# Three mixed pairs of K tiles instead of two in the MLP's up products

## The chip, the cores and the metric

The kernel runs on one core of one Trainium2 chip. The metric is the device time of one execution in microseconds (us); the time of a kernel is the median of its runs. Three runs of the kernel before took 2447.22, 2447.89 and 2448.03 us, so its time is 2447.89 us. One more execution was recorded by the hardware profiler; it is the source of every row of the profile below.

## The reference

A decoder of two layers over 256 tokens of width 2048, all in float32. Each layer has an attention, an MLP and a gated embedding step, each behind an RMSNorm. The change touches the MLP alone:

```python
hn = rmsnorm(h, mlp_norm_g[i])
h = h + jnp.square(jax.nn.relu(hn @ mlp_w1[i])) @ mlp_w2[i]
```

`mlp_w1[i]` is 2048 x 8192 and `mlp_w2[i]` is 8192 x 2048. The first product is called the ups here, the second the downs.

## The kernel before

**Every product in three.** A float32 operand is split into a part rounded to the matmul's format (hi) and the remainder (lo). A product of two operands is the sum of three matmuls: hi x hi, lo x hi, hi x lo (`terms`). In the rows below, `xa` holds the split activations of one K tile (128 features by 256 tokens, hi and lo side by side), `whi` and `wlo` the split weights of one chunk, `h` the split hidden activations. TensorE (PE) takes 128 tokens of an activation tile as its stationary operand and streams 512 weight columns through it, so each matmul row reads 128x512. Three such matmuls are one block product, called a triple from here on.

**Chunks.** Weights come as chunks of 128x1024 (512 KB), two K tiles by 512 columns. `Program.run` walks a list of chunks and writes the instructions of each engine in order. Of each chunk SyncE (SP) issues the load into `raw` (4 buffers), ScalarE (ACT) casts it to `whi` (line 243, 6 buffers), and VectorE (DVE) subtracts to get `wlo` (line 251, 5 buffers). Casts are written up to four chunks ahead of the matmuls, subtractions three (`SPLIT_AHEAD`). Each engine works its list in order, so an instruction that waits holds everything behind it on that engine. A subtraction waits for its cast, and for PE to be done with the chunk five places back, whose `wlo` buffer it takes; a load waits until the buffer of the load four places back was read for the last time.

**The MLP.** `mlp` cuts the 8192 hidden columns into 4 blocks (`NFB`) of four groups of 512. The first two groups of block 0 are made by `ups` on their own, chunk by chunk (`token_major`, line 589). All other groups are made two at a time by `up_mixed` (`pair_major`, line 493): seven calls in a layer, fourteen in the kernel. The calls of block 0 stand alone, the others come in two right behind each other, and downs stand between the blocks.

**Plain and mixed pairs.** A call of `up_mixed` handles groups 0 and 1, each with eight chunks, one for each pair of K tiles. A pair that is plain costs two chunks of four triples: two K tiles by two halves of the tokens, for each group. A pair in `MIXED` costs seven triples for both groups together, after Strassen's scheme in Winograd's form. It is worked as four items named a, b, t and u of two, one, two and two triples. Items a and b are loaded chunks. Item t takes the sum `ts` that DVE makes of both chunks (line 531), and item u what DVE makes of them in place in b's `raw` buffer (lines 536 and 537); both are then cast and subtracted like a loaded chunk, b only in half. The buffer of a is free again after line 536, that of b after the subtraction of u. The mixed items also need sums of the pair's activations, the tile `xf`, made once in a layer for each mixed pair by `x_forms` (ACT at 553 and 563, DVE at 556 to 559 and 566; `all_forms`). Four banks of PSUM collect the extra products of a call; after the last mixed item `sums` combines them (lines 778 to 783), and each group's `done` adds its own bank (line 790) before the squared ReLU. `turned` then brings the rows into feature order through DRAM: DVE transposes blocks (line 697), SP writes `dU` and reads it back into `w` in four parts, ACT and DVE split it to `h` (lines 757 and 759).

**The order.** `order` in `up_mixed` is written by hand. Before, with M for a mixed pair, 0 and 1 for a plain chunk of that group, a call reads 0 0 M 0 1 0 M 0 0 1 1 1 1 1: twenty items. `all_forms` is started behind the last chunk of the first `ups`.

**A scratch tile.** `rsh` (32 partitions by 256) is scratch of the rotary embedding in three places; it comes from the pool `tmp`, which stays open throughout.

Of the kernel before, what the change touches and what calls it, by code (L numbers as in the profile page):

```python
# [10 lines left out]
F32 = mybir.dt.float32  # L11
F32R = mybir.dt.float32r
# [3 lines left out]
P = 128  # L16
D = 2048
T = 256
# [16 lines left out]
DMA_AHEAD = 7  # L35
SPLIT_AHEAD = 3
RAW_BUFS, HI_BUFS, LO_BUFS = 4, 6, 5
MIXED = (2, 5)

G_ATTN, G_MLP, G_PLE, G_KV, G_FIN = 0, 2, 4, 6, 7  # L40

# [119 lines left out]
def kernel(ctx: ExitStack, tc: tile.TileContext, a: dict, out: bass.AP):  # L161
# [386 lines left out]
    def x_forms(k, gi, to):  # L548


        u = [tmp.tile([P, T], F32, tag="sq", name="sq", bufs=3) for _ in range(3)]
        for i in range(2):
            nc.scalar.activation(u[i], x[k + i], AF.Identity, scale=gain(gi, k + i))
        yield
        a, b, s = u
        nc.vector.tensor_sub(s[:, :P], a[:, P:], b[:, P:])
        nc.vector.tensor_sub(s[:, P:], a[:, :P], a[:, P:])
        nc.vector.tensor_sub(a[:, :P], a[:, :P], s[:, :P])
        nc.vector.tensor_sub(b[:, :P], b[:, :P], a[:, :P])
        f = cur["z"].tile([P, 2, 2 * T], F32R, tag="xf", name="xf", bufs=2)  # L560
        parts = ((slice(0, T), s), (slice(T, T + P), a[:, :P]), (slice(T + P, 2 * T), b[:, :P]))
        for c, v in parts:
            nc.scalar.copy(f[:, 0, c], v)
        yield
        for c, v in parts:
            nc.vector.tensor_sub(f[:, 1, c], v, f32(f[:, 0, c]))
        to[k // 2] = f
# [29 lines left out]
    def to_head(ps, norm, dst, roped, mark, late=0, lo=None):  # L597

        t = sum_halves(ps)
        for _ in range(1 + late):  # L600
            yield
        while norm.r is None:
            yield
        if callable(dst):
            dst = dst()
        elif dst is None:
            dst = t
        if not roped:
            nc.vector.tensor_mul(dst, t, norm.rb)
        else:  # L610
            sh = tmp.tile([32, T], F32, tag="rsh", name="rsh", bufs=2)
            nc.vector.stream_shuffle(sh, t[:32, :], ROPE_SWAP)
            nc.vector.tensor_mul(dst, t, norm.rc)
            nc.vector.tensor_mul(sh, sh, norm.rs)
            nc.vector.tensor_add(dst[:32, :], dst[:32, :], sh)
        if lo is not None:
            yield
            nc.scalar.copy(lo[0], dst)
            yield
            nc.vector.tensor_sub(lo[1], dst, f32(lo[0]))  # L620
        mark()
# [19 lines left out]
            out[-1].append(s)  # L641
        return out

    def taken_late(f, g, ops=()):

        both = [by_chunk(prog.collect(p)) for p in (f, g)]
        for c in range(0, KT // 2, 2):
            if c == KT // 2 - 2:
                for fn in ops:
                    prog.op(fn)  # L650
            for steps in both:
                prog.steps += steps[c] + steps[c + 1]

    def out_proj(src, nk, oT, gi, to, norm, hooks, twos, close):

# [70 lines left out]
    def mlp(layer, xg, norm, to, norm2, opening):  # L726
# [45 lines left out]
        def up_mixed(b, q):  # L772

            ts = []

            def sums(aux):
                s, o = row(), row()
                nc.scalar.copy(s[:, 0], aux["P1"])
                yield
                nc.vector.tensor_sub(s[:, 1], aux["R6"], s[:, 0])  # L780
                nc.vector.tensor_add(o[:, 0], aux["Q5"], s[:, 1])
                nc.vector.tensor_sub(s[:, 1], aux["Q7"], s[:, 1])
                nc.vector.tensor_sub(o[:, 1], o[:, 0], aux["Q7"])
                ts.extend((s, o))

            def done(i, ps):
                while not ts:
                    yield
                t = ts[i]
                nc.vector.tensor_add(t, ps, t)  # L790
                for j in range(2):
                    nc.scalar.activation(t[:, j], t[:, j], AF.Relu, scale=norm.col[:, j:j + 1])
                yield from up(b, q + i, t)

            plain_ = [c for c in range(KT // 2) if c not in MIXED]
            c0, c1, c2, c3, c4, c5 = plain_
            order = [(0, c0), (0, c1), MIXED[:1], (0, c2), (1, c0), (0, c3), MIXED[1:], (0, c4), (0, c5)] + \
                [(1, c) for c in plain_[1:]]
            pair_major(lambda i, c: a["w1"][layer * 128 + (b * 4 + q + i) * 8 + c], order, xg, forms, sums, done)

        def normed(k):
# [24 lines left out]
        def downs(b, q):  # L826
            token_major(chunks("w2", b, q), hid[b], lambda *ps: down(b, q, *ps), whole=True)

        taken_late(lambda: ups(0, 0, {4: [lambda: norm.factor(rows=True)]}), lambda: ups(0, 1), opening)
        def all_forms():  # L830
            for c in MIXED:
                yield from x_forms(2 * c, G_MLP + layer, forms)
                yield
        prog.op(all_forms)
        for b in range(NFB):
            for q in range(0, 4, 2):
                if b or q:
# [536 lines left out]
    def key_unit(n, i, which, at, hooks=None):  # L1374

        def done(ps0, ps1, mm):
# [3 lines left out]
            for g in range(GB):  # L1380
# [2 lines left out]
                k4, c4, s4 = (v.rearrange("p (j a r) -> p j a r", j=2, a=4) for v in  # L1383
                              (cur["E"].tile([P, T], F32, tag="et", name="et", bufs=7), n_b1.rc, n_b1.rs))
                src = w.rearrange("p a (g j r) -> p g j a r", j=2, r=32)[:, g]
                sh = tmp.tile([32, T], F32, tag="rsh", name="rsh", bufs=2)
                sh4 = sh.rearrange("p (j a r) -> p j a r", j=2, a=4)
                nc.vector.tensor_mul(k4, src, c4)
                nc.vector.stream_shuffle(sh4, src[:32], ROPE_SWAP)
# [215 lines left out]

    def q_done(h, ps):
        t = sum_halves(ps)
        sh = tmp.tile([32, T], F32, tag="rsh", name="rsh", bufs=2)
        nc.vector.stream_shuffle(sh, t[:32, :], ROPE_SWAP)
        nc.vector.tensor_mul(t, t, n_b1.rc)  # L1610
        nc.vector.tensor_mul(sh, sh, n_b1.rs)
# [245 lines left out]
```

## Time and profile before

| | |
|---|---|
| median of three runs | 2447.89 us (2447.22 to 2448.03) |
| the profiled execution: its own time | 2447.25 us |
| the profiled execution: span, first to last instruction | 2445.5 us |
| VectorE (DVE) busy | 1774.0 us, 73% of the span |
| ScalarE (ACT) busy | 1371.5 us, 56% |
| DMA | 532.26 MB, mean 218 GB/s |

So 1.75 us of the profiled execution lie outside its span. The page of the profile gives busy times by engine, the chain of work that ended last, and the costliest groups of instructions. A row of the view by groups reads: line, engine, operation, tiles (written <- read), shape, count, then busy us and mean ns of one, then the idle time of the engine just before these instructions with what ended it. A row of the timeline reads: start, length (of x instructions that follow each other), engine, line, operation. A matmul's length is longer than its distance to the next, since matmuls overlap; distances between starts are what counts. PEld rows are the loads of stationary operands.

### The profile page before, as it was taken

To read this page: it belongs to the slowest core of one execution; us is meant where nothing else is said; L and a number is where in the kernel's file an instruction comes from. 1 tells how busy PE (TensorE), PEld (TensorE's weight loads), DVE (VectorE), ACT (ScalarE), POOL (GpSimd) and SP (SyncE) were. 2 spreads that over 40 slices of the span, in tenths; PEclk is the share of its full clock that TensorE was granted. 3 is DMA by queue.
4 is the path that set the end of the run, shared out by engine and by line. 5 is a ranking of instruction groups with operands and counts; after the bars stand their busy time and mean duration, and the time that the engine had idled before them with its cause. 6 is when DMAs were issued, how large, how long until landed. Compare 5 with 4: busy or idle time off the path is not lost.

```text
span 2445.5 us, 33009 instructions
## 1 busy us (share of the span) xinstructions
PE 2434.5 (100%) x11763; PEld 2050.8 (84%) x11763; DVE 1774.0 (73%) x2666; ACT 1371.5 (56%) x1997; POOL 10.3 (0%) x24
## 2 busy tenths in 40 slices
PE   9999999999999999999999999999999999999998
PEld 8888888888888888888888889988888888888887
DVE  7866687776585675777678989867658668567766
ACT  6544444565464454564564788756545546445556
POOL 0000000000000000000100000000000000000000
PEclk9999999999999999999999999999999999999999
DMA  7666665767577576687776743476857757758775
GB/s 276 201 214 215 196 210 197 223 222 249 182 240 235 190 250 220 194 271 241 243 242 210 256 165 121 141 226 219 262 182 233 240 186 239 233 187 257 247 233 161
DMA packets 174981, 532.26 MB, mean 218 GB/s; under 512 B 19616, under 2 KB 51808, under 8 KB 174816
## 3 DMA queue, kind: packets, MB, share of 16 engines
q1 hardware_dynamic: 173712, 528.30, 66.3%
q8 instruction: 92, 1.51, 0.2%
q0 software_dynamic: 528, 1.07, 0.1%
q10 hardware_dynamic: 576, 0.79, 0.1%
q14 instruction: 73, 0.60, 0.1%
HBM read 496.00 MB, written 34.08 MB: 217 GB/s over the span
## 4 chain that ended last, share of the span: by engine, by line
PE 99%; DVE 0%; DMA 0%; ACT 0%; SPq 0%; issue 0%; ACTq 0%; DVEq 0%
PE at L589 26%; PE mm L589 25%; PE at L493 21%; PE mm L384 11%; PE mm L386 6%; PE mm L493 3%; PE at L384 1%; PE at L386 1%; PE at L1682 1%; PE mm L1706 0%; PE mm L1446 0%; PE mm L916 0%; PE mm L918 0%; PE mm L917 0%; PE mm L1447 0%; PE at L1167 0%
## 5 line engine op out<-in xcount | busy, mean ns | idle before, releaser
L251 DVE TENSOR_TENSOR wlo<-raw,whi 128x1024 fp32r<-128x1024 f32 (+1 forms) x903 | 1075.8, 1199 | 500.3 <-PE mm L589 151.3
L243 ACT CAST whi<-raw 128x1024 fp32r<-128x1024 f32 (+1 forms) x903 | 930.5, 1039 | 727.2 <-PE mm L589 207.6
L493 PE MATMUL at<-whi,xa 128*128 128x512 f32 x1456 | 448.2, 389 | 0.0
L384 PE MATMUL mm<-xa,whi 128*128 128x512 f32 x1104 | 371.7, 395 | 0.0
L493 PEld LDWEIGHTS at<-whi,xa 128*128 128x128 f32 x1456 | 273.3, 188 | 56.8
L589 PE MATMUL mm<-whi,h 128*128 128x512 f32 x1024 | 315.2, 389 | 0.0
L589 PE MATMUL at<-whi,h 128*128 128x512 f32 x1024 | 315.2, 389 | 0.0
L493 PE MATMUL at<-wlo,xa 128*128 128x512 f32 x728 | 283.2, 389 | 0.0
L386 PE MATMUL mm<-xa,wlo 128*128 128x256 f32 x1104 | 273.3, 278 | 0.0
L589 PEld LDWEIGHTS at<-whi,h 128*128 128x128 f32 x1024 | 192.2, 188 | 39.9
L589 PEld LDWEIGHTS mm<-whi,h 128*128 128x128 f32 x1024 | 192.2, 188 | 39.9
L386 PEld LDWEIGHTS mm<-xa,wlo 128*128 128x128 f32 x1104 | 207.3, 188 | 18.0
L384 PEld LDWEIGHTS mm<-xa,whi 128*128 128x128 f32 x1104 | 193.3, 188 | 30.5 <-issue 0.4
L589 PE MATMUL at<-whi,xa 128*128 128x512 f32 x672 | 208.0, 391 | 1.5 <-DVE et L392 1.3
L589 PE MATMUL mm<-whi,xa 128*128 128x512 f32 x656 | 202.8, 390 | 0.0
L589 PE MATMUL mm<-wlo,h 128*128 128x512 f32 x512 | 199.2, 389 | 0.0
L589 PE MATMUL at<-wlo,h 128*128 128x512 f32 x512 | 199.2, 389 | 0.0
L493 PEld LDWEIGHTS at<-wlo,xa 128*128 128x128 f32 x728 | 136.6, 188 | 28.3
L589 PEld LDWEIGHTS at<-whi,xa 128*128 128x128 f32 x672 | 125.2, 189 | 26.9 <-issue 1.4
L589 PEld LDWEIGHTS mm<-whi,xa 128*128 128x128 f32 x656 | 122.5, 188 | 25.1
L589 PE MATMUL at<-wlo,xa 128*128 128x512 f32 x336 | 130.6, 390 | 0.2 <-DVE wlo L251 0.2
L589 PE MATMUL mm<-wlo,xa 128*128 128x512 f32 x328 | 127.7, 389 | 0.0
(405 smaller groups left out, 2698.5 us busy)
## 6 DMA issues: line engine op xcount, KB each, us to landing
raw<-in_w SPq DMA_DIRECT2D x512, 512.0 KB, 4.4
raw<-in_w_qk SPq DMA_DIRECT2D x96, 512.0 KB, 3.7
raw<-in_w_gate SPq DMA_DIRECT2D x64, 512.0 KB, 4.3
raw<-in_w_kv SPq DMA_DIRECT2D x48, 512.0 KB, 4.4
raw<-in_w_v SPq DMA_DIRECT2D x47, 512.0 KB, 4.4
dU<-z SPq DMA_DIRECT2D x46, 512.0 KB, 4.2
w<-dU SPq DMA_DIRECT2D x184, 128.0 KB, 5.0
raw<-in_w_q SPq DMA_DIRECT2D x32, 512.0 KB, 4.2
```

Of the source, the lines that this page charges most:

```text
L243: nc.scalar.copy(hi[:, c], t[:, c])
L251: nc.vector.tensor_sub(lo[:, c], t[:, c], f32(hi)[:, c])
L384: nc.tensor.matmul(ps, hi[:, col:col + P], rhs, start=first, stop=False)
L386: nc.tensor.matmul(ps[:, :T], lo[:, col:col + P], rhs[:, :T], start=False, stop=last)
L493: nc.tensor.matmul(ps, x_, w_, start=b not in touched, stop=end and last[b] == n and i == 2)
L589: nc.tensor.matmul(st[j], *parts[j][i], start=k == i == 0, stop=k == kt - 1 and i == 2)
L1682: nc.tensor.transpose(tr[:, i * P:(i + 1) * P], src, ident)
```

## The change

`MIXED` has three pairs, 1, 3 and 5, where it had 2 and 5. The order of a call becomes 0 0 M 0 1 M 0 1 M 0 1 1 1, 22 items. The activations' sums are started two chunks earlier: `taken_late` interleaves the two `ups` by two chunks, and `all_forms` now starts between the last two chunks of the first and the last two of the second. `xf` has three buffers. `rsh` moves from `tmp` to the pool `E`. The host-side layout of `w1` swaps the two column groups in the mixed chunks, and follows `MIXED` by itself.

```diff
-MIXED = (2, 5)
+MIXED = (1, 3, 5)
...
-        f = cur["z"].tile([P, 2, 2 * T], F32R, tag="xf", name="xf", bufs=2)
+        f = cur["z"].tile([P, 2, 2 * T], F32R, tag="xf", name="xf", bufs=len(MIXED))
...
-            sh = tmp.tile([32, T], F32, tag="rsh", name="rsh", bufs=2)
+            sh = cur["E"].tile([32, T], F32, tag="rsh", name="rsh", bufs=2)
...
-    def taken_late(f, g, ops=()):
+    def taken_late(f, g, ops=(), mid=()):
...
-            for steps in both:
+            for n, steps in enumerate(both):
                 prog.steps += steps[c] + steps[c + 1]
+                if c == KT // 2 - 2 and n == 0:
+                    for fn in mid:
+                        prog.op(fn)
...
-            plain_ = [c for c in range(KT // 2) if c not in MIXED]
-            c0, c1, c2, c3, c4, c5 = plain_
-            order = [(0, c0), (0, c1), MIXED[:1], (0, c2), (1, c0), (0, c3), MIXED[1:], (0, c4), (0, c5)] + \
-                [(1, c) for c in plain_[1:]]
+            c0, c1, c2, c3, c4 = [c for c in range(KT // 2) if c not in MIXED]
+            m0, m1, m2 = [(c,) for c in MIXED]
+            order = [(0, c0), (0, c1), m0, (0, c2), (1, c0), m1, (0, c3), (1, c1), m2,
+                     (0, c4), (1, c2), (1, c3), (1, c4)]
...
-        taken_late(lambda: ups(0, 0, {4: [lambda: norm.factor(rows=True)]}), lambda: ups(0, 1), opening)
         def all_forms():
             for c in MIXED:
                 yield from x_forms(2 * c, G_MLP + layer, forms)
                 yield
-        prog.op(all_forms)
+        taken_late(lambda: ups(0, 0, {4: [lambda: norm.factor(rows=True)]}), lambda: ups(0, 1), opening,
+                   [all_forms])
```

The first place where rows move is the start of the first mixed call of a layer, on DVE. Before, its rows from the subtraction of the second plain chunk to the first mixed item's rows; `sq` and `xf` are the activations' sums, `pg` is other work:

```order
L251 TENSOR_TENSOR wlo<-raw,whi 128x1024 x2
L626 TENSOR_TENSOR pg<-ps,pg 128x256
L531 TENSOR_TENSOR ts<-raw 128x1024
L251 TENSOR_TENSOR wlo<-raw,whi 128x512
L697 STREAM_TRANSPOSE z<-t 128x2x4x4x32
L556 TENSOR_TENSOR sq<-sq 128x128
L557 TENSOR_TENSOR sq<-sq 128x128
L558 TENSOR_TENSOR sq<-sq 128x128
L559 TENSOR_TENSOR sq<-sq 128x128
L536 TENSOR_TENSOR raw<-ts,raw 128x512
L537 TENSOR_TENSOR raw<-raw 128x512
```

And the same place now:

```order
L251 TENSOR_TENSOR wlo<-raw,whi 128x1024
L556 TENSOR_TENSOR sq<-sq 128x128
L557 TENSOR_TENSOR sq<-sq 128x128
L558 TENSOR_TENSOR sq<-sq 128x128
L559 TENSOR_TENSOR sq<-sq 128x128
L251 TENSOR_TENSOR wlo<-raw,whi 128x1024
L626 TENSOR_TENSOR pg<-ps,pg 128x256
L566 TENSOR_TENSOR xf<-sq,xf 128x256
L566 TENSOR_TENSOR xf<-sq,xf 128x128 x2
L531 TENSOR_TENSOR ts<-raw 128x1024
L251 TENSOR_TENSOR wlo<-raw,whi 128x512
L700 STREAM_TRANSPOSE z<-t 128x2x4x4x32
```

The first pair's activation sums have moved ahead of `ts`; those of the second pair now stand where those of the first stood, behind the first mixed item, and those of the third where those of the second stood. (Line numbers behind the edits are three higher in the changed kernel.)

The second place is the second of two calls that follow each other, on DVE, between its first and its second mixed pair. Before, from the transposition of the call ahead to the second pair's `ts`:

```order
L697 STREAM_TRANSPOSE z<-t 128x2x4x4x32
L251 TENSOR_TENSOR wlo<-raw,whi 128x1024
L759 TENSOR_TENSOR h<-w,h 128x4x4x32
L251 TENSOR_TENSOR wlo<-raw,whi 128x1024
L759 TENSOR_TENSOR h<-w,h 128x4x4x32
L251 TENSOR_TENSOR wlo<-raw,whi 128x1024 x2
L531 TENSOR_TENSOR ts<-raw 128x1024
L251 TENSOR_TENSOR wlo<-raw,whi 128x512
```

Now:

```order
L700 STREAM_TRANSPOSE z<-t 128x2x4x4x32
L251 TENSOR_TENSOR wlo<-raw,whi 128x1024 x3
L762 TENSOR_TENSOR h<-w,h 128x4x4x32
L531 TENSOR_TENSOR ts<-raw 128x1024
L251 TENSOR_TENSOR wlo<-raw,whi 128x512
L762 TENSOR_TENSOR h<-w,h 128x4x4x32
L536 TENSOR_TENSOR raw<-ts,raw 128x512
```

One subtraction fewer stands between the pairs, and the splits of the hidden activations of the call ahead (`h`) have moved from among the plain chunks into the second mixed pair.

More of the change, by code (lines that the diff above doesn't have):

```diff
@@ L1385, in done @@
                 src = w.rearrange("p a (g j r) -> p g j a r", j=2, r=32)[:, g]
-                sh = tmp.tile([32, T], F32, tag="rsh", name="rsh", bufs=2)
+                sh = cur["E"].tile([32, T], F32, tag="rsh", name="rsh", bufs=2)
                 sh4 = sh.rearrange("p (j a r) -> p j a r", j=2, a=4)
@@ L1607, in q_done @@
         t = sum_halves(ps)
-        sh = tmp.tile([32, T], F32, tag="rsh", name="rsh", bufs=2)
+        sh = cur["E"].tile([32, T], F32, tag="rsh", name="rsh", bufs=2)
         nc.vector.stream_shuffle(sh, t[:32, :], ROPE_SWAP)
```

## The prediction

> **What bounds the kernel now.** I read the page first: busy times, the granted clock, and the chain of work that ended last.
>
> ```profile
> span 2445.5 us, 33009 instructions
> ...
> PE 2434.5 (100%) x11763; PEld 2050.8 (84%) x11763; DVE 1774.0 (73%) x2666; ACT 1371.5 (56%) x1997; POOL 10.3 (0%) x24
> ...
> PEclk9999999999999999999999999999999999999999
> ...
> PE 99%; DVE 0%; DMA 0%; ACT 0%; SPq 0%; issue 0%; ACTq 0%; DVEq 0%
> ```
>
> TensorE (PE) is busy over the whole span at an undiminished clock, and the chain is PE from end to end. Since matmuls overlap in the rows, a full PE need not be a PE at its pace, so the timeline of PE inside a mixed call comes next. A row with x2 holds the first two matmuls of a block product, the row behind it the third.
>
> ```profile
> 902.51 0.61 PE L493 MATMUL at<-whi,xa 128*128 128x512 f32 x2
> 902.96 0.39 PE L493 MATMUL at<-wlo,xa 128*128 128x512 f32 x1
> 903.19 0.61 PE L493 MATMUL at<-whi,xa 128*128 128x512 f32 x2
> ```
>
> From 902.51 to 903.19 is 0.68 us for a block product, 0.2267 us a matmul. The view by windows says whether that pace holds through a call; its columns are start and end, length, busy time of PE, PEld, DVE, ACT and POOL, clock, DMA share and GB/s. The first window is the mixed call that stands alone in layer 0, the second two calls in a row.
>
> ```profile
> 518.99:561.31 42.32, 42.32 (x188) 35.07 (x187) 35.64 (x47) 28.70 (x38) 0.00 (x0) 1.00 0.70 234
> 648.19:732.67 84.48, 84.48 (x374) 69.98 (x373) 66.78 (x67) 50.73 (x57) 0.00 (x0) 1.00 0.69 225
> ```
>
> A call has 6 plain pairs of 8 block products and 2 mixed of 7: 62, and 62 x 0.68 = 42.16 us; two calls make 84.32. The windows are 0.16 longer, the overhang of the last matmul. No time is lost on PE in these calls, so a block product less is worth its full 0.68 us as long as PE is still fed. DVE has 6.7 us free in the first window and 17.7 us in the second.
>
> The Trainium skill (Perfetto Trace Analysis, section Identifying the Most-Contended Engine) says that matmul busy time does not tell how near TensorE is to its roof, and to go by the busy share of the weight loads. By that share, 84%, a sixth of PE would be open and removing products might free nothing; the even distance of 0.68 us speaks against it here.
>
> **What is removed on PE.** The number of calls follows from the matmuls on activation sums, four block products or 12 matmuls in each mixed pair.
>
> ```profile
> L493 PE MATMUL mm<-whi,xf x168: 389/389/389, 526.5 to 2227.6; 128*128 128x512 f32 x168
> L493 PE MATMUL mm<-wlo,xf x84: 389/389/389, 526.9 to 2227.8; 128*128 128x512 f32 x84
> ...
> L493 PE MATMUL at<-whi,xf x56: 389/389/389, 525.1 to 2224.8; 128*128 128x512 f32 x56
> ...
> L493 PE MATMUL at<-wlo,xf x28: 389/389/389, 525.6 to 2225.1; 128*128 128x512 f32 x28
> ```
>
> 168 + 84 + 56 + 28 = 336 = 14 calls x 2 pairs x 12. These matmuls last as long as those on plain activations, 389 ns, so a mixed pair has no dearer products, only one fewer. One more mixed pair in 14 calls removes 14 x 0.68 = **9.52 us**. The Trainium skill (TensorE: Matmul & The Clock Gate, section Back-to-back issue gap) gives 216 ns for a lone matmul of 512 columns and 131 ns in a sustained stream; 42 matmuls would by that be worth 9.1 or 5.5 us, an estimate from that page. The distance in this trace is 227 ns, and I use that.
>
> **What is added on DVE and ACT.** The view by groups over the second window has the means of one.
>
> ```profile
> L251 DVE TENSOR_TENSOR wlo<-raw,whi 128x1024 fp32r<-128x1024 f32 x33 | 39.3, 1217 | 14.9 <-ACT whi L243 9.1 <-PE at L493 5.6
> L251 DVE TENSOR_TENSOR wlo<-ts,whi 128x1024 fp32r<-128x1024 f32 x4 | 4.9, 1218 | 0.7 <-PE at L589 0.7
> ...
> L531 DVE TENSOR_TENSOR ts<-raw 128x1024 f32<-128x1024 f32 x3 | 3.7, 1223 | 0.2 <-DMA raw<-in_w 0.2
> ...
> L537 DVE TENSOR_TENSOR raw<-raw 128x512 f32<-128x512 f32 x3 | 2.1, 691 | 0.1
> L536 DVE TENSOR_TENSOR raw<-ts,raw 128x512 f32<-128x512 f32 x3 | 2.1, 684 | 0.0
> L251 DVE TENSOR_TENSOR wlo<-raw,whi 128x512 fp32r<-128x512 f32 x3 | 2.0, 683 | 0.0
> ```
>
> A mixed pair costs DVE 3 x 1.22 for a, t and u, 0.68 for b, 1.22 for `ts`, 0.68 + 0.69 for u's sums: 6.93 us. The two plain chunks it replaces cost 2.43. That is 4.5 us more in each call, 63 us in all, beside 4.76 us of PE in the mixed pair. It costs nothing while DVE's free time covers it: 9.0 of 17.7 us where two calls follow each other, 4.5 of 6.7 in a call that stands alone. ACT gets one and a half casts more, about 1.6 us a call, beside 13.6 us free in the first window. No byte more is loaded. `rsh` is written and read by DVE alone, so in `E` it waits for nothing new; I cost it at nothing, and a wait there would have to show outside the MLP.
>
> Averages don't decide, because DVE runs ahead by no more than its buffers allow and is caught up with inside a mixed pair. What decides is how long before its use `wlo` is ready. The next rows are DVE's and PE's at the start of the first call.
>
> ```profile
> 511.09 1.23 DVE L251 TENSOR_TENSOR wlo<-raw,whi 128x1024 fp32r<-128x1024 f32 x1 [1.16 <-issue]
> 513.81 1.22 DVE L251 TENSOR_TENSOR wlo<-raw,whi 128x1024 fp32r<-128x1024 f32 x1 [1.49 <-ACT pg L624]
> ```
> ```profile
> 524.88 0.39 PE L493 MATMUL mm<-wlo,xa 128*128 128x512 f32 x1
> ```
>
> Item a of the first mixed pair is ready at 515.03 and used at 524.88: 9.85 us ahead, as far as it gets. The gaps of 1.2 and 1.5 us are where the first pair's activation sums, about 2 us, now go. The tight place is the second mixed pair of the same call:
>
> ```profile
> 529.44 2.35 DVE L251 TENSOR_TENSOR wlo<-raw,whi 128x1024 fp32r<-128x1024 f32 x2
> ...
> 533.73 1.23 DVE L531 TENSOR_TENSOR ts<-raw 128x1024 f32<-128x1024 f32 x1 [1.34 <-DMA raw<-in_w]
> ...
> 536.08 0.69 DVE L536 TENSOR_TENSOR raw<-ts,raw 128x512 f32<-128x512 f32 x1
> ...
> 537.41 1.22 DVE L251 TENSOR_TENSOR wlo<-ts,whi 128x1024 fp32r<-128x1024 f32 x1
> ...
> 539.14 1.22 DVE L251 TENSOR_TENSOR wlo<-raw,whi 128x1024 fp32r<-128x1024 f32 x1
> 540.28 0.68 DVE L759 TENSOR_TENSOR h<-y,h 128x512 fp32r<-128x512 f32 x1
> 540.88 3.49 DVE L251 TENSOR_TENSOR wlo<-raw,whi 128x1024 fp32r<-128x1024 f32 x3
> ```
> ```profile
> 541.20 0.39 PE L493 MATMUL mm<-wlo,xf 128*128 128x512 f32 x1
> ...
> 542.56 0.39 PE L493 MATMUL at<-wlo,xa 128*128 128x512 f32 x1
> ```
>
> Item u is ready at 539.14 + 1.22 = 540.36 and used at 541.20, with 0.84 us in hand; the chunk behind it at 540.88 + 1.22 = 542.10 for 542.56, 0.46 in hand. Now three things change. PE comes one plain chunk earlier: 4 x 0.68 = 2.72 us. DVE has one subtraction fewer on the way: 1.13. Two sets of activation sums lie on the way as before. And the wait of 1.34 us for the second loaded chunk goes, wholly or nearly, since its load now takes the buffer that the first pair's u frees, one place earlier in SP's list and ahead of the transfers of `w`. If it goes, u is ready at 540.36 - 1.13 - 1.34 = 537.9 for 538.48; if it stays, at 539.2, which is 0.7 late. I take 538.2, nearer to the first: 0.3 in hand, and the chunk behind it, 1.74 us later for DVE and 1.36 for PE, 0.1 late.
>
> To the third pair's u DVE then has two `h` (0.60 each from start to start: 540.28 to 540.88), two plain chunks and a (1.14 each: 539.14 to 540.28), `ts` 1.14, b 0.60, lines 536 and 537 with 1.33 (536.08 to 537.41), t and u 1.14 each: 9.97 us. PE has 15 block products, 10.2 us. So it holds, with next to nothing in hand, if the loads come in time:
>
> ```profile
> raw<-in_w SPq DMA_DIRECT2D x512, 512.0 KB, 4.4
> ```
> ```profile
> 527.10 0.43 SPq L231 DMA_DIRECT2D raw<-in_w  x1
> ```
>
> The third pair's second chunk is issued when u frees the buffer, at 538.2, and lands 4.4 us later at 542.6; DVE wants it at 538.2 + 2 x 0.60 + 3 x 1.14 = 542.8. But the load issued at 527.10, among the transfers of `dU`, was awaited until 533.73, 6.6 us. That would be 2.0 late, of which 0.5 is in hand: 1.5 us. So the stall in this call lies between nothing and 0.7 + 1.5 = 2.2 us. I take **0.4**, near the first end, for the row that fits is the median; it comes once in each layer: 0.8.
>
> Where two calls follow each other, the second is the tighter one: its DVE list is held up by line 790, which waits for the call ahead.
>
> ```profile
> 690.55 1.23 DVE L790 TENSOR_TENSOR t<-at,t 128x1024 f32<-128x1024 f32 x1 [1.90 <-PE at L493]
> ...
> 697.53 1.18 DVE L251 TENSOR_TENSOR wlo<-raw,whi 128x1024 fp32r<-128x1024 f32 x1
> ...
> 708.33 1.22 DVE L251 TENSOR_TENSOR wlo<-raw,whi 128x1024 fp32r<-128x1024 f32 x1
> ```
> ```profile
> 712.56 0.39 PE L493 MATMUL mm<-wlo,xf 128*128 128x512 f32 x1
> ```
>
> The second pair's u is ready at 709.55 for 712.56, 3.0 in hand. Now DVE has from 697.53 on three subtractions (two plain, a), one `h`, `ts`, b, one `h`, 1.33, and t before u: 3 x 1.14 + 0.60 + 1.14 + 0.60 + 0.60 + 1.33 + 1.14 = 8.83, so u is ready at 706.36 + 1.22 = 707.6, for 712.56 - 2.72 = 709.84: 2.3 in hand. The third pair, 9.97 against 10.2 as above, leaves it there. Twelve of the 14 calls should thus run without a stall.
>
> **The sum.** 2447.25 (the profiled execution) - 9.52 + 0.8 = 2438.5. The median of the runs is 0.64 above the profiled execution, so **2439.2 us**.
>
> **The rivals.** *A: the load comes late in both single calls.* The row for it is 527.10; against it, the median of 512 loads. 2.2 instead of 0.4 us twice: 2439.2 + 3.6 = 2442.8.
>
> *B: DVE becomes the bound in every call.* This one ends slower. Its place is the third mixed pair, its point where DVE's work and those of its waits that don't shrink pass PE's time. ACT's waits for loads are the ones that may stay:
>
> ```profile
> L243 ACT CAST whi<-raw 128x1024 fp32r<-128x1024 f32 x34 | 35.0, 1052 | 17.6 <-DMA raw<-in_w 9.0 <-PE at L493 6.4 <-DVE raw L537 0.9
> ```
>
> In two calls DVE would need 66.78 + 9.0 + 9.0 + 1.90 (line 790) = 86.7 us, and PE 84.48 - 1.36 = 83.1. DVE's lead when it enters, up to 9.85 us, covers these 3.6; should the buffers make it worth nothing, it costs 6 x 3.6, and as much again per call in the two single ones, 2 x 1.8: 25.2 us, so 2447.89 - 9.52 + 25.2 = 2463.6. It passes the time before by 0.2% from about 1.0 us a call. For it: 92% busy is little room. Against it: much of the idle time ends with PE, and such waits shrink by themselves when DVE falls behind.
>
> *C: PE is not what the time hangs on,* and the products removed turn into waits: 2447.9. Against it stands the even 0.68. That the products aren't removed at all is no rival, since PE's list is 42 matmuls shorter.
>
> **How the numbers follow.** A measurement of this kernel can tell 0.2%, 4.9 us, from no change. My forecast has 0.72, A 0.14 (0.03 of it within 0.2%), B 0.09 (0.06 slower, 0.03 within), C 0.05. So faster 0.83, within 0.2% 0.11, slower 0.06. The range starts at the lowest run without a stall, 2447.2 - 9.5 = 2437.7, rounded down to 2437.5, and reaches over A to 2443.5, which leaves B and C out.
>
> **What would show it.** PE must have 11763 - 42 = 11721 matmuls, a single call must take 61 x 0.68 + 0.16 = 41.64 us, two in a row 83.12, with what goes beyond as stall. In the first call u of the second and third pair should be ready within half a microsecond of its use; elsewhere 2 us ahead. DVE's busy time should rise by some 63 us, ACT's by 24. Wrong would be: PE rows at line 493 with idle time before them in the calls that follow each other (B), over 1 us of it in the single calls (A), or calls as long as before at a wider distance between block products (C).

## The result and the profile after

The changed kernel takes 2461.95 us (median of four runs, 2459.71 to 2464.73), beside 2447.72 us for the kernel before (2447.22 to 2448.03). The ratio is 1.0059, with a 95% interval of 1.0041 to 1.0076: it is 14.2 us slower, though 42 matmuls are gone. The prediction was 2439.2, in a range of 2437.5 to 2443.5. From the lowest to the highest of the four runs, the mean granted clock falls from 0.999 to 0.997.

The page of the changed kernel, the lines that answer to those of before:

```profile
span 2459.8 us, 33103 instructions
...
PE 2433.7 (99%) x11721; PEld 2041.2 (83%) x11721; DVE 1835.4 (75%) x2750; ACT 1393.1 (57%) x2035; POOL 10.4 (0%) x24
...
PE 94%; DVE 2%; DMA 1%; ACT 1%; issue 1%; SPq 0%; ACTq 0%; DVEq 0%
```

The matmuls are as few as forecast, but the chain that ended last is no longer PE from end to end: DVE, DMA and ACT now hold it up. The view by windows, one row for each stretch of mixed calls, tells where (columns as in the prediction; rows of 41.6 us are single calls, the others two calls in a row):

```profile
519.25:560.89 41.64, 41.64 (x185) 34.51 (x184) 38.66 (x53) 26.53 (x37) 0.00 (x0) 1.00 0.74 240
647.77:734.20 86.43, 84.36 (x368) 68.48 (x367) 71.81 (x74) 49.33 (x57) 0.00 (x0) 1.00 0.63 213
821.08:908.34 87.26, 84.36 (x368) 68.51 (x367) 74.26 (x78) 48.33 (x54) 0.00 (x0) 1.00 0.63 211
995.22:1082.17 86.95, 84.54 (x368) 68.46 (x367) 74.25 (x78) 48.19 (x54) 0.00 (x0) 1.00 0.63 212
1698.30:1739.95 41.65, 41.65 (x185) 34.52 (x184) 38.76 (x53) 26.86 (x38) 0.00 (x0) 1.00 0.74 240
1826.82:1915.47 88.65, 85.59 (x368) 69.50 (x367) 72.08 (x74) 50.21 (x58) 0.00 (x0) 0.98 0.63 207
2002.34:2088.93 86.59, 84.34 (x368) 68.48 (x367) 74.16 (x78) 48.15 (x54) 0.00 (x0) 1.00 0.64 213
2175.81:2262.27 86.46, 84.29 (x368) 68.48 (x367) 73.64 (x78) 47.70 (x54) 0.00 (x0) 1.00 0.64 213
```

The single calls run at PE's pace: 61 x 0.68 + 0.16 = 41.64. Two calls in a row should take 83.12; the six take 86.43 to 88.65, together 23.6 us too much. The longest is the one row with a granted clock of 0.98 and not 1.00: right behind a wait of PE the clock was 0.50 for 3.41 us (1892.64 to 1896.05), which makes about 1.5 of the 23.6 us. With the 9.5 us saved that is +14.1, and the two spans differ by 14.3. So the whole of it lies in these six stretches. In each, the distances between matmuls are even in the first call. Added up over the second calls (what each distance between matmuls over 240 ns has beyond 227), 6.1 us are lost at the first mixed pair and the chunk behind it, 16.7 us from the second mixed pair on; the 1.5 us of half clock are among the latter.

### The profile page after: what moved, and what is told of

It is laid out like the page before. It is cut to its first block, busy times and chain, and to the rows that moved or that the text cites. A ratio compares the mean times of both kernels' runs of the same rounds, so it can differ in the third digit from the quotient of the medians.

```text
span 2459.8 us, 33103 instructions
## 1 busy us (share of the span) xinstructions
PE 2433.7 (99%) x11721; PEld 2041.2 (83%) x11721; DVE 1835.4 (75%) x2750; ACT 1393.1 (57%) x2035; POOL 10.4 (0%) x24
## 4 chain that ended last, share of the span: by engine, by line
PE 94%; DVE 2%; DMA 1%; ACT 1%; issue 1%; SPq 0%; ACTq 0%; DVEq 0%
PE at L589 26%; PE mm L589 25%; PE at L493 16%; PE mm L384 11%; PE mm L386 6%; PE mm L493 4%; PE at L384 1%; DVE wlo L251 1%; DMA w<-dU 1%; ACT whi L243 1%; PE at L386 1%; PE at L1685 1%; PE mm L1709 0%; DVE z L700 0%; DVE ts L531 0%
## 5 line engine op out<-in xcount | busy, mean ns | idle before, releaser
L493 PE MATMUL at<-whi,xa 128*128 128x512 f32 x1288 | 398.5, 391 | 7.0 <-ACT whi L243 7.0
L493 PEld LDWEIGHTS at<-whi,xa 128*128 128x128 f32 x1288 | 242.0, 188 | 59.1 <-ACT whi L243 9.6
L493 PE MATMUL at<-wlo,xa 128*128 128x512 f32 x644 | 252.6, 392 | 6.7 <-DVE wlo L251 6.7
L589 PE MATMUL at<-whi,xa 128*128 128x512 f32 x672 | 207.6, 390 | 1.7 <-DVE et L392 1.3
L493 PEld LDWEIGHTS at<-wlo,xa 128*128 128x128 f32 x644 | 121.3, 188 | 36.8 <-DVE wlo L251 11.9
L589 PEld LDWEIGHTS at<-whi,xa 128*128 128x128 f32 x672 | 124.6, 188 | 27.4 <-issue 1.4
L589 PE MATMUL at<-wlo,xa 128*128 128x512 f32 x336 | 130.8, 390 | 0.3 <-DVE wlo L251 0.3
```

The costliest lines, as they stand in the source:

```text
L493: nc.tensor.matmul(ps, x_, w_, start=b not in touched, stop=end and last[b] == n and i == 2)
L589: nc.tensor.matmul(st[j], *parts[j][i], start=k == i == 0, stop=k == kt - 1 and i == 2)
```

## What the trace shows at the handover

In what follows the *tail* is the chunks behind a call's last mixed pair, the *finish* of a group is its addition (line 790, now 793) with the activations behind it, and the second call's start is where PE ends the first: 61 triples or 41.48 us after the window's start, 62 or 42.16 in the kernel before. DVE's timeline of before, around the finishes of both groups of a first call (second call's start: 819.55 + 42.16 = 861.71), then ACT's row of the first finish:

```profile
849.07 1.22 DVE L790 TENSOR_TENSOR t<-at,t 128x1024 f32<-128x1024 f32 x1
850.20 1.21 DVE L251 TENSOR_TENSOR wlo<-raw,whi 128x1024 fp32r<-128x1024 f32 x1
853.79 1.23 DVE L251 TENSOR_TENSOR wlo<-raw,whi 128x1024 fp32r<-128x1024 f32 x1 [2.38 <-ACT whi L243]
...
861.91 1.22 DVE L790 TENSOR_TENSOR t<-at,t 128x1024 f32<-128x1024 f32 x1 [1.76 <-PE at L493]
```
```profile
850.38 1.34 ACT L792 ACTIVATE t<-t,col 128x512 f32<-128x512 f32 x2 [2.04 <-DVE t L790]
```

And of the changed kernel (second call's start: 821.08 + 41.48 = 862.56), DVE, then ACT:

```profile
857.06 1.22 DVE L793 TENSOR_TENSOR t<-at,t 128x1024 f32<-128x1024 f32 x1
858.20 1.21 DVE L251 TENSOR_TENSOR wlo<-raw,whi 128x1024 fp32r<-128x1024 f32 x1
861.77 1.23 DVE L251 TENSOR_TENSOR wlo<-raw,whi 128x1024 fp32r<-128x1024 f32 x1 [2.36 <-ACT whi L243]
...
865.18 0.68 DVE L251 TENSOR_TENSOR wlo<-raw,whi 128x512 fp32r<-128x512 f32 x1
865.78 1.22 DVE L793 TENSOR_TENSOR t<-at,t 128x1024 f32<-128x1024 f32 x1
...
870.43 1.23 DVE L251 TENSOR_TENSOR wlo<-raw,whi 128x1024 fp32r<-128x1024 f32 x1 [0.97 <-ACT whi L243]
871.58 1.24 DVE L700 STREAM_TRANSPOSE z<-t 128x1024 f32<-128x1024 f32 x1
872.74 2.32 DVE L251 TENSOR_TENSOR wlo<-raw,whi 128x1024 fp32r<-128x1024 f32 x2
```
```profile
858.37 1.34 ACT L795 ACTIVATE t<-t,col 128x512 f32<-128x512 f32 x2 [3.05 <-DVE t L793]
859.74 1.06 ACT L752 ACTIVATE t<-t 128x1024 f32<-128x1024 f32 x1
860.71 1.55 ACT L243 CAST whi<-raw 128x1024 fp32r<-128x1024 f32 x2
```

The 2.4 us for which DVE waits behind a finish are in both kernels: ACT stands at the activation, which needs DVE's addition (2.04 us before, 3.05 now), and the casts that DVE needs next are queued behind it. Before, this was paid 12.6 us ahead of the second call, and DVE had caught up when PE ended the first one: it even waited 1.76 us for PE. Now it is paid 5.5 us ahead, and the second group's addition starts 3.2 us behind PE instead of waiting for it. The subtraction behind the first mixed pair starts at 872.74, 10.18 us after the second call's start. The row that the prediction took for it, 697.53, stood at 697.53 - (648.19 + 42.16) = 7.18. PE is held there:

```profile
873.97 0.50 PE L493 MATMUL at<-wlo,xa 128*128 128x512 f32 x1 [0.58 <-DVE wlo L251]
...
882.52 0.50 PE L493 MATMUL mm<-wlo,xf 128*128 128x512 f32 x1 [0.78 <-DVE wlo L251]
886.14 0.73 PE L493 MATMUL at<-whi,xa 128*128 128x512 f32 x2 [1.01 <-ACT whi L243]
887.40 0.50 PE L493 MATMUL at<-wlo,xa 128*128 128x512 f32 x1 [0.53 <-DVE wlo L251]
```

The later rows are at the second mixed pair and the chunk behind it. There two queues wait for the second group's `w`. SP's rows and DVE's:

```profile
880.03 1.75 SPq L200 DMA_DIRECT2D w<-dU  x4
881.83 2.28 SPq L231 DMA_DIRECT2D raw<-in_w  x3
```
```profile
879.33 0.68 DVE L762 TENSOR_TENSOR h<-w,h 128x512 fp32r<-128x512 f32 x1
...
885.17 0.69 DVE L762 TENSOR_TENSOR h<-w,h 128x512 fp32r<-128x512 f32 x1 [1.42 <-ACT h L760]
```

The one buffer `w` is free when the first group's last `h` is made, at 879.33 + 0.68 = 880.01. At 880.03 SP reads `dU` into it, with three loads of weights behind; DVE then stands 1.42 us for the `h` made of it, with the subtractions for PE behind.

## Experiments

First, which call's third pair does it, and do the small edits cost anything? **Three pairs in the first of two calls only (e1), or in the second only (e2)** (single calls always three; the calls with two have the order of before):

```diff
+            if b == 0 or q == 0:      # the other run: if q == 2
                 order = [(0, c0), (0, c1), m0, (0, c2), (1, c0), m1, (0, c3), (1, c1), m2, ...]
+            else:
+                order = [(0, c0), (0, c1), m0, (0, c2), (1, c0), (0, c3), m1, (0, c4), (0, c5)] + ...
```

> Three mixed pairs in the two single calls and in the first of each two calls, two pairs in the order of before in the second: 8 block products fewer than before, 8 x 0.68 = 5.4 us. Theory H (handover): the first call's shorter tail, four chunks behind its last mixed pair with 8.16 us between the finishes of its two groups instead of 13.6, lets DVE enter the second call some 3 us late; then the second call stalls though it has only two pairs, by at least the 2 us of its first pair: windows of two calls of 85.8 us or more where 83.80 is stall-free, time 2454 to 2466 us. Theory D (density): the second call's own three pairs are what DVE can't keep up with; then windows of 83.80 and 2447.7 - 5.4 = 2442.3 us. Theory S (loads held on SP behind the transfers of dU and w): as H, since those transfers lie in the second call.

> Three mixed pairs in the two single calls and in the second of each two calls, two pairs in the order of before in the first: again 8 block products fewer, 5.4 us. Theory H: the first call keeps its long tail, DVE enters the second call as before, no stall: windows of 83.80 us, time 2442.3. Theory D: the second calls stall as in the changed kernel, 3.3 to 5.5 us each: time 2442.3 + 23.6 = 2465.9. Theory S: the transfers of dU and w come at other places against the loads, so some stall less than D.

Measured: 2461.58 with three in the first calls (ratio 1.0055, 1.0042 to 1.0067), 2442.28 with three in the second calls (0.9976, 0.9966 to 0.9986). The first window of two calls in each, e1 then e2, where 83.80 is free of a stall:

```profile
648.13:734.50 86.37, 85.08 (x371) 69.05 (x370) 69.47 (x71) 51.44 (x58) 0.00 (x0) 1.00 0.65 211
```
```profile
647.51:731.32 83.81, 83.81 (x371) 69.44 (x370) 67.66 (x69) 49.12 (x56) 0.00 (x0) 1.00 0.68 220
```

Three pairs in the second call cost nothing; three in the first make the second call lose 3.0 us on average, though that has only two. Theory D falls, and the forecast 2442.3 of H is met.

**The small edits alone (e3)**, two pairs as before:

> The kernel before with two mixed pairs, with only the activations' sums started two chunks earlier and rsh in pool E. All theories: as before, 2447.7 within 1 us, windows of the calls 42.32 and 84.48. If it is over 1 us slower, a part of the 14.2 us lies in these two edits and not in the calls.

Measured 2447.67 beside 2448.34 (0.9998, 0.9989 to 1.0007). They cost nothing.

**The transfers on another queue (e4):**

```diff
-        nc.sync.dma_start(d, src)
+        nc.gpsimd.dma_start(d, src)
...
-            nc.sync.dma_start(to[32 * b:32 * b + 32], d4[b])
+            nc.gpsimd.dma_start(to[32 * b:32 * b + 32], d4[b])
```

> The changed kernel, with the MLP's hidden activations' transfers to dU and back to w issued by GpSimd instead of SyncE, so that the loads of weights no longer queue behind them. Theory S: the stalls of the second calls go wholly or for the most part: 2438.2 to 2446 us. Theories H and D: the stall at the head of the second calls (about 2 us each, 12 in all) has no such load in it and stays; 2450 to 2462 us.

Measured 2518.17 (1.0283, 1.0269 to 1.0297). Loads no longer queue behind the transfers, but `w` comes later still, and DVE stands 4.3 to 6.1 us for `h` in each second call. No theory's range holds this time. Theory S isn't met, but neither are H and D, since the run made a new wait; it is taken up below.

Then the order of the first calls alone is changed, with three pairs in all calls:

```
changed kernel   0 0 M 0 1 M 0 1 M 0 1 1 1
e5               0 0 M 0 1 M 0 M 0 1 1 1 1
e6               0 0 M 0 0 M 0 M 1 1 1 1 1
e8               0 0 M 0 M 0 M 0 1 1 1 1 1
e9               0 M 0 M 0 M 0 0 1 1 1 1 1
e7, two pairs    0 0 M 0 1 0 1 0 1 M 0 1 1 1
```

The last is the other way round: the kernel before, with its two pairs, gets a short tail.

> Three mixed pairs in every call; in the first of each two calls alone the third pair comes one plain chunk earlier (0 0 M 0 1 M 0 M 0 1 1 1 1), so the finishes of its two groups lie four chunks or 10.9 us apart, not 8.16 as in the changed kernel and not 13.6 as before. Theory H (handover): DVE is 1.6 us less late at the second call (2.72 us of PE less 1.14 of DVE in a plain chunk), so about 1.6 to 2.4 us of the 3.9 us a second call loses on average go: 2447 to 2453 us. Rival W (work: the third pair's 4.5 us on DVE in the first call make it late, wherever they stand): 2462.

> Three mixed pairs in every call; in the first of each two calls the order is 0 0 M 0 0 M 0 M 1 1 1 1 1, so group 0 finishes with the last mixed item and group 1 five chunks or 13.6 us later, the distance of before. Theory H: DVE enters the second call on time, windows of two calls 83.12 us, time 2447.7 - 9.5 = 2438.2, up to 2441 if the one plain chunk between the second and third pair is too few. Rival W: 2462.

> The kernel before with its two mixed pairs and 62 block products, but in the first of each two calls two plain chunks move from behind the last mixed pair to ahead of it (0 0 M 0 1 0 1 0 1 M 0 1 1 1), so that the finishes of the two groups lie 8.16 us apart as in the changed kernel. Theory H: slower though nothing is computed otherwise; the windows of two calls, 84.48 now, grow by about the 2.6 to 3.8 us that the run with three pairs in the first calls alone lost: 2447.7 + 18 = 2466 us, at least 2455. Rival W: as before, 2447.7.

> Three mixed pairs in every call; in the first of each two calls one plain chunk between the pairs and a tail of six (0 0 M 0 M 0 M 0 1 1 1 1 1), so group 0 finishes one chunk behind the last mixed pair and group 1 five chunks or 13.6 us later. Theory H: as with group 0 first, 2438.2 us, up to 2444 if one plain chunk between the pairs is too few for DVE (a pair costs it 6.9 us and a plain chunk 1.14, where PE takes 4.76 and 2.72, so it loses 0.6 us of its lead with each, but starts with up to 9.85). Rival W: 2462 or more, since the pairs stand closer.

> Three mixed pairs in every call; the first of each two calls has the order 0 M 0 M 0 M 0 0 1 1 1 1 1, so seven chunks follow its last mixed pair, as many as before. Theory H as the run with group 0 first has corrected it (that run had 13.6 us between the finishes and still lost 1.7 us a call, as the one with 10.9 did, and both have five chunks behind the last mixed pair): what counts is how many chunks follow the last mixed pair, since sums and the first finish stand on DVE two chunks behind it: 3.8 us lost with four, 1.7 with five, 0.5 with six, nothing with seven. So windows of 83.12 us and 2438.2 us, up to 2439.5. Rival W (the pairs' work, wherever it stands): not below the 2441.1 of the run with one chunk between the pairs, since DVE has one chunk less ahead of the first pair here.

| run | pairs in the first call | tail, chunks | lost in a second call, mean | time (before beside it) |
|---|---|---|---|---|
| e7 | 2 | 4 | 2.8 us | 2464.16 (2448.04) |
| changed kernel | 3 | 4 | 3.9 us | 2461.95 (2447.72) |
| e5 | 3 | 5 | 1.7 us | 2449.74 (2448.04) |
| e6 | 3 | 5 | 1.7 us | 2450.15 (2448.04) |
| e8 | 3 | 6 | 0.6 us | 2441.12 (2448.04) |
| e9 | 3 | 7 | 0 | 2438.35 (2447.99) |
| kernel before | 2 | 7 | 0 | 2447.72 |

The loss is the window's length over PE's pace. In e7 and in the changed kernel one of the six windows holds an interval at half clock, some 0.3 us of the mean. The kernel before, with nothing but three plain chunks moved (the expectation says two; the order has three fewer in the tail), becomes as slow as the changed kernel. A window of it, where 84.48 was the length before:

```profile
822.59:909.67 87.08, 85.71 (x374) 69.71 (x373) 67.50 (x69) 48.64 (x54) 0.00 (x0) 1.00 0.64 208
```

DVE is busy 67.5 us of 87; in the same two calls of the kernel before (819.55 to 904.03) it was 68.4 of 84.5. So rival W falls: it isn't the third pair's work. Run e6 was a miss: its finishes lie 13.6 us apart on PE, and it still loses as much as e5. Both have five chunks of tail. The sums of a call, which both finishes need, stand on DVE two steps behind the last mixed pair, whatever the order of the groups; in e6 the first addition starts 6.8 us ahead of the second call, as in e5, and not 13. So the tail counts, not the distance of the finishes, and e9, made after this correction, came out at the number expected. Its window and its second addition (second call's start 648.22 + 41.48 = 689.70):

```profile
648.22:731.34 83.12, 83.12 (x368) 68.85 (x367) 71.74 (x74) 50.01 (x58) 0.00 (x0) 1.00 0.69 222
...
689.90 1.23 DVE L793 TENSOR_TENSOR t<-at,t 128x1024 f32<-128x1024 f32 x1
```

With 2438.35 us (ratio 0.9960, 0.9948 to 0.9973) e9 is faster than both kernels: 9.6 us under the kernel before, where 42 matmuls were worth 9.52.

Last, what joins a short tail to PE's stall? These keep the changed kernel's order. One writes the sums and additions a step sooner (a step is one chunk), one makes the second group's `h` two steps later, one has the activations a step behind the addition:

```diff
                 nc.scalar.copy(s[:, 0], aux["P1"])
-                yield                                       # e10
...
             w = yield from turned(t, ...)
+            for _ in range(late):                           # e11: 2 for the first call's second group
+                yield
...
                 nc.vector.tensor_add(t, ps, t)
+                yield                                       # e12
                 for j in range(2):
                     nc.scalar.activation(t[:, j], t[:, j], AF.Relu, scale=norm.col[:, j:j + 1])
```

> The changed kernel and its order, but all DVE rows of the sums and the first group's finish are written one chunk sooner behind the last mixed pair. Corrected H: it acts like a fifth chunk behind the pair, 1.7 instead of 3.8 us lost in a second call: about 2449.7 us, 2445 to 2453. If only the time between the finishes on PE counted, or DVE's work as such, nothing would change: 2462. DVE now waits for ACT's copy, which may cost it up to 1 us a call.

> The changed kernel and its order, but the casts and subtractions that make h for the second group of the first call are written two chunks later. The changed kernel loses 6.1 us in all at the first mixed pair of the second calls and 16.7 at the second. Theory T (transfers): the latter is DVE and ACT waiting in order for h, whose way through dU and w starts 3 us late: those waits of 1.3 to 2.3 us on DVE go, and most of the 16.7: 2445 to 2450 us. Rival C (capacity): DVE has too much to do at that place and waits there cost nothing: 2460 to 2464.

> The changed kernel and its order, but in each finish the activations on ACT behind DVE's addition are written one chunk later, so that ACT doesn't stand waiting for that addition with casts behind it. Theory A (ACT's order): the idle time of 2.4 and 1.0 us that DVE spends waiting for casts behind the two finishes goes, DVE is on time at the second call's first pair, and the 6.1 us lost there go: 2450 to 2457 us. Rival T: all that follows comes a chunk later, so h too, and what is gained at the first pair is lost at the second: 2460 to 2475.

All three missed in time: 2466.24 (1.0076, 1.0064 to 1.0089), 2465.77 (1.0075, 1.0061 to 1.0089) and 2463.53 (1.0058, 1.0045 to 1.0071). In e10 DVE reaches the sums sooner and waits there for ACT's copy, which stands behind a cast that waits for a load. Its rows on DVE and ACT:

```profile
856.39 0.69 DVE L782 TENSOR_TENSOR t<-mm,t 128x512 f32<-128x512 f32 x1 [2.02 <-ACT t L781]
```
```profile
854.83 1.05 ACT L243 CAST whi<-raw 128x1024 fp32r<-128x1024 f32 x1 [1.71 <-DMA raw<-in_w]
855.78 0.58 ACT L781 COPY t<-mm 128x512 f32<-128x512 f32 x1
```

In e12 DVE's second addition comes 0.9 to 1.5 us behind the second call's start and not over 3.2, and nothing is lost at the first mixed pair of any second call; but `h` comes a step later too, and 3.0 to 4.4 us are lost from the second pair on. So ACT's order is behind the loss at the first pair, as theory A has it. Rival T is right that `h` is late: DVE waits 2.9 to 3.6 us for the second group's, where the changed kernel's waits 1.3 to 2.3. But that is not all of the loss. In five of the six stretches PE's clock was halved for 3.41 us behind such a wait. DVE's row, the window of such an interval, and PE's rows in it:

```profile
888.15 0.69 DVE L762 TENSOR_TENSOR h<-w,h 128x512 fp32r<-128x512 f32 x1 [3.55 <-ACT h L760]
```
```profile
890.52:893.93 3.41, 3.41 (x9) 2.65 (x10) 3.41 (x5) 1.16 (x3) 0.00 (x0) 0.50 0.50 156
```
```profile
890.87 1.05 PE L493 MATMUL at<-whi,xa 128*128 128x512 f32 x2
...
892.15 1.05 PE L493 MATMUL at<-whi,xa 128*128 128x512 f32 x2
```

A block product takes 1.28 us there and not 0.68. Of the 23.4 us that e12 loses from the second pair on, some 7.9 fall in these intervals; the other 15.5 are about what the changed kernel loses there at full clock, 16.7 - 1.5 = 15.2. So the trace does not show that the later `h` alone undoes the gain. What e12 would take at full clock is open: its sixth stretch, without such an interval, loses 3.0 us, 1.15 of them at the third pair, where PE waits for nothing in the other five.

In e11 the wait for `h` on DVE is gone, but another stands in its place. DVE's row and SP's:

```profile
890.97 1.23 DVE L251 TENSOR_TENSOR wlo<-raw,whi 128x1024 fp32r<-128x1024 f32 x1 [3.76 <-ACT whi L243]
```
```profile
876.47 0.33 SPq L231 DMA_DIRECT2D raw<-in_w  x1
882.36 1.75 SPq L200 DMA_DIRECT2D w<-dU  x4
884.15 0.91 SPq L231 DMA_DIRECT2D raw<-in_w  x2
```

From 876.80 to 882.36 SP issues nothing; a load that DVE's next chunk needs goes out at 884.15, behind the transfer that waited for `w`. So one wait holds two queues, and an edit that frees one leaves the other. Four runs tried both at once, with the transfers on GpSimd: with all `h` later (e13), that and the activations later (e14), and the same two with only the second group's `h` later (e15, e16).

> The changed kernel and its order, with two edits at once that did nothing good alone: the MLP's transfers to dU and back to w are issued by GpSimd, not SyncE, and the casts and subtractions that make h from w are written two chunks later, for all groups. Theory T2: the loss at the second mixed pair of the second calls (2.2 to 4.5 us each) is the in-order wait for the second group's w, which stands twice, on SP ahead of the loads and on ACT and DVE ahead of casts and subtractions; take away one and the other still holds. With both gone that loss falls below 1 us a call, and only the 1 us at the first pair stays: two-call windows of 84.2 to 85.2, time 2445 to 2451. Rival C (capacity of DVE at the second pair): windows of 86 us and more as in the changed kernel, 2459 us or more.

> As the run before, and the activations of each finish on ACT are written one chunk later as well, which alone took away the loss at the first mixed pair and made that at the second larger. Theory T2 with A (ACT's order): no loss is left at either pair, though all of the order is that of the changed kernel with four chunks behind the last mixed pair: windows of 83.1 to 84 us, 2438 to 2444 us. Rival C: 2455 us or more.

> As the run with transfers on GpSimd and all h two chunks later, but h is later for the second group alone (and for the second of the plain ups). In that run no time was lost at the second mixed pair any more (68.5 us for the first 297 matmuls of two calls, 1.0 over their pace, all at the first pair), but 4 to 6 us ahead of the third: h of the first group, made later, freed the one buffer w later, and w of the second group came back only after that. Theory T2: with the first group's h in its old place that goes too, and 1 us at the first pair of each second call stays: windows of 84.2 to 85.5, time 2445 to 2452. Rival C (capacity): windows of 86 us and more, 2459 us or more.

> As the run before, and the activations of each finish on ACT a chunk later. With all h later this lost nothing in the first 303 matmuls of two calls, both mixed pairs included (68.84 us, their pace exactly). Theory T2 with A: windows of 83.1 to 84.5 us, 2438 to 2446 us, with four chunks behind the last mixed pair. Rival C: 2455 us or more.

They missed as well: 2542.99, 2517.12, 2498.50 and 2480.71 us. In the first, 1.0 to 2.0 us are lost in a second call up to the third mixed pair, and in the second nothing: the second pair is clear, or nearly so. But `w` is slow on that queue (ACT went on 9.2 us after its issue at 714.23 in e14, where the changed kernel's went on 4.5 us after 880.03), so in all four time is lost at the third pair, and outside the mixed calls they take 40, 9, 31 and 4 us more than the kernel before. Half clock takes its part too: these runs have five to thirteen intervals of it, of 3.4 to 10.2 us, and e4 eight. These runs could not tell the wait for `w` from a lack of room on DVE. Leaving the transfer out can (e17, and e18 with the activations later; in both, `h` of the groups whose transfer is left out is not the reference's):

```diff
+        if stay:                        # first call's second group
+            for _ in range(4):
+                yield
+            return z.rearrange("p (a n) -> p a n", a=4)
         w = new("w").rearrange("p (a n) -> p a n", a=4)
         g = bounce(z, "dU", w)
```

> The changed kernel and its order, but the second group of each first call leaves out its way through dRAM: its h is made from z, where its transposed blocks stand, at the same places of ACT's and DVE's lists, so six writes of dU and 24 reads into w are not issued, and h of those groups is not the reference's. All DVE, ACT and PE work stays. Theory T2 (the wait for w on two queues is the loss at the second mixed pair): that loss goes from 2.2 to 4.5 us to under 0.5 in each second call, the 1 us at the first pair stays: windows of 84 to 84.8, time 2444 to 2448. Rival C (DVE's capacity or its lateness as such): windows of 86 us and more, 2456 to 2462.

> As the run before, with the same transfers left out, and the activations of each finish on ACT written one chunk later, which alone cleared the first mixed pair. Theory T2 with A: no loss is left: windows of 83.1 to 83.5, 2438 to 2441 us. Rival C: 2452 us or more.

Measured: 2450.05 (1.0008, 0.9999 to 1.0017) and 2438.90 (0.9962, 0.9950 to 0.9974). The first is some 2 us above its range: from the second pair on 0.4 to 1.4 us stay lost in a call, at the first pair 1.0 to 1.5. With the activations later as well, five of the six stretches take 83.12 us and one 83.46. A window of each:

```profile
993.09:1077.93 84.84, 84.19 (x368) 68.54 (x367) 74.15 (x78) 48.17 (x55) 0.00 (x0) 1.00 0.64 205
```
```profile
817.64:900.76 83.12, 83.12 (x368) 68.85 (x367) 73.65 (x78) 49.04 (x55) 0.00 (x0) 1.00 0.65 209
```

The last has the short tail, all three pairs and all of DVE's work, 73.65 us in the window beside 74.26 in the changed kernel's, and PE doesn't wait in it. Rival C falls: DVE has room for three pairs. Leaving out the transfers also leaves less to move, but the loads of weights land hardly sooner for it: their median is 4.4 us in e17 and 4.3 in e18, beside 4.4 in the changed kernel. What held PE were, but for the 1.5 us of half clock, two waits in order, one on ACT, one for `w`, that a short tail moves into the second call's mixed pairs.

## Why the prediction was wrong, point by point

- **What bounds the kernel, and what a product is worth:** right. PE was the bound, and e9 gained 9.6 us for the 9.52 of 42 matmuls. Rival C of the prediction fell with it, and so did the reading of the weight loads' share as room on PE; the 131 ns that the Trainium skill (TensorE: Matmul & The Clock Gate, section Back-to-back issue gap) gives for a stream would, as an estimate from that page, have made this 5.5 us; the measured distance was 227 ns.
- **The added work:** right in size. DVE's busy time rose by 61.4 us (63 forecast), ACT's by 21.6 (24). The early sums and `rsh` cost nothing, as e3 shows.
- **The single calls:** right but for 0.4 us each: 41.64 and 41.65 us without a stall. The late load, rival A, did not come there. In the profiles of other runs with the transfers on SP the single call of the first layer took up to 1.7 us more, once with two pairs too (43.38 for 42.32 in e3). In e11, with the 1.7 us, and in e3 ACT stood there 1.71 and 2.57 us for the transfer of `y`, which in that call is what `w` is elsewhere, ahead of casts (0.49 us in the changed kernel); so a late transfer can hold this call too, and 41.64 was in part luck.
- **The second of two calls:** here it failed, at the step "Now DVE has from 697.53 on three subtractions". That start was taken from the trace of before, as if DVE came to the second call as it did then. The forecast counted what the new order does within a call, but not that it leaves four chunks behind the last mixed pair, where there were seven. That is 8.16 us less of PE's time for the sums, both finishes and the waits behind them. DVE was 10.18 us into the second call at that row and not 7.18, which is more than the 2.3 us "in hand". "Twelve of the 14 calls should thus run without a stall" became eight.
- **What a wait does behind it:** the prediction knew that a wait holds up a list (line 790 on DVE, the transfers of `w` on SP), but in the second call it gave each `h` its bare 0.60 us and put the wait for the second group's `w` at nothing. Without that transfer (e17) 3.7 of the 16.7 us from the second pair on were left, so this wait, on SP, ACT and DVE, makes over half of the loss.
- **Rival B** came within 2 us of the time, 2463.6, by another way. It put the loss at the third pair and into all calls, because DVE's work would exceed PE's time. The loss lies at the first and second pair of second calls. With the same work on DVE, e9 loses nothing in any of the six stretches and e18 0.3 us in one. That the number fits is luck.

Shown by runs: that the tail sets the loss (e1, e2, e5, e7, e8, e9), that ACT's order makes the loss at the first pair (e12, and e17 against e18), that the second group's transfer makes most of the rest (e17, e18). Not separated: how much of that rest is SP's held loads and how much the wait for `h`, since e4 and e11 each freed one and the other took its place; and how much of e12's loss from the second pair on is the half clock.

## What to carry to other kernels

When the order of a piece is rewritten, work out where each engine stands when it leaves the piece, too: a margin read from the old trace holds only if the engine enters there as before. Work that ends a piece (sums, activations, a transfer) needs cover by plain work behind it, and moving dense items towards the end takes that cover from the next piece. An engine that is 89% busy (DVE in e18, 73.65 of 83.12 us) can have room enough, and one that is 85% busy (74.26 of 87.26 in the changed kernel) can stall the bound engine through what is queued behind a wait; look at such waits, not at the share.

## What was not expected of the hardware

Issued by GpSimd, the same transfers took longer. The rows of DMA issues (KB each, median us to landing) of the changed kernel and of e4:

```profile
dU<-z SPq DMA_DIRECT2D x46, 512.0 KB, 4.0
```
```profile
dU<-z POOLq DMA_DIRECT2D x30, 512.0 KB, 6.2
```

The Trainium skill (DMA: Bandwidth & Descriptors, section Issuing engine by pattern) says that the path of the sync and scalar engines is generally faster; these rows agree. Of the 46 writes of the changed kernel, the 30 that e4 moves to GpSimd took 4.1 us, so the difference is 2.1 us for a write of 512 KB. Each issue of it took GpSimd 0.56 us, and SP 0.33.

The granted clock fell to one half for 3.41 us at a time in some of the kernels in which PE waits. Leaving out the end of each kernel and the runs with transfers on GpSimd, the profiled executions show it once in the changed kernel, in e7 and in e10, and five times in e12. Each of these eight intervals begins within 1.0 us behind the start of a matmul that had waited. There is none in the kernel before, e2, e3, e9 and e18, where PE loses 1.1 us at most in a call or two in a row; there is also none in e1, e5, e6, e8, e11 and e17, where it loses more. So a wait can cost more than its own length. The length of the wait alone doesn't decide it: in e12 waits of 1.15 and 0.70 us shortly behind each other (up to 1896.7) were followed by such an interval, in e10 waits of 1.36 and 0.70 us (up to 890.0) were not.
